# Parameter loads on other queues, wider statistics products, more start-up transposes and an earlier group-A output in a mixer + mixture-of-experts block

## The chip, the core and the metric

The kernel runs on one core of a Trainium2 chip. The metric is device time in microseconds (us) of one execution. A core has five engines that run their own instruction lists in order and wait for each other by semaphores: TensorE (PE, matmuls; its weight loads are shown as PEld), VectorE (DVE), ScalarE (ACT), GpSimd (POOL) and SyncE (SP, which here only issues DMAs). ACT and POOL can issue DMAs too. All DMAs share 16 DMA engines.

## The reference

One encoder layer over 256 tokens of 1024 channels, all in float32. What matters here is the first half, up to the output projection, and that 32 experts' weights (192 MB) have to be read in the second half.

```python
def mixer_block(h, w_in, conv_a_w, conv_b_w, conv_b_bias, ln_b_g, ln_b_b, beta_a, beta_b, w_out):
    proj = jnp.einsum("bsd,dc->bsc", h, w_in)
    a_in, a_b, a_c, b_val, b_gate = jnp.split(proj, ..., axis=-1)
    y_a = a_b * depthwise_conv_centred(a_c * a_in, conv_a_w)          # width 3
    u = b_val * jax.nn.sigmoid(b_gate)
    u = depthwise_conv_centred(u, conv_b_w) + conv_b_bias             # width 31
    y_b = jax.nn.silu(layernorm(u, ln_b_g, ln_b_b))
    y = jnp.concatenate([head_rmsnorm(y_a, N_HEADS_A, beta_a),
                         head_rmsnorm(y_b, N_HEADS_B, beta_b)], axis=-1)
    return jnp.einsum("bsc,cd->bsd", y, w_out)

h = rmsnorm(x, norm_mix_g);  x = x + mixer_block(h, ...)
h = rmsnorm(x, norm_ffn_g);  x = x + hierarchical_moe(h, ...)   # 4 groups of 8 experts, top 1 group, top 2 experts
return rmsnorm(x, norm_final_g)
```

## The kernel before

Channels lie on the 128 partitions, tokens along the free axis, so each of the two groups has four blocks (`b` = 0 to 3) of 128 channels by 256 tokens. The order of every engine's work is the order in which the code is written; nothing is rearranged.

**Weights.** A ring of 25 buffers of 1 MB holds all weights. `stream` lists the transfers in the order of use; `fill()` issues them on SP as long as buffers are free, and `done()` gives buffers back with a rank. Besides the buffers, each DMA of SP and ACT takes the next of eight completion lanes, and waits until the DMA eight places before it has landed.

**Start.** `x` comes in two halves (one DMA on ACT, one on SP). PE turns identity matrices into a scratch tile (line 226, 14 times) and then transposes the 16 blocks of `x` (line 235). The row norm is made by DVE, ACT and two more transposes (line 239), then `keep_busy(15)` issues 15 more identity transposes (line 216) while DVE forms the normalised `hT` (line 243). The parameters of the convolutions and norms (31 rows of `conv_b_w`, 3 of `conv_a_w`, 5 single rows) are loaded into `prow`, which shares memory with `vb`, and are transposed into `prm` by line 388.

**Projections.** `proj()` makes one block: plain float32 for the first (`g` and `v`, line 298), otherwise a split into a high and a low part (lines 302, 303 and 307), for which ACT makes the high parts of the weights (`split_hi`, line 270) and POOL the low ones (`split_lo`, line 276, 10 times). Block order on PE: g0, v0, g1, v1, g2, v2, g3, v3 (group B), then c, i and b of group A.

**Group B's wide convolution** runs on DVE: 31 taps (line 338, one multiply-add each) for every block; for the last block ten of the taps are done by ACT (multiply, line 323) and POOL (add, line 325), handed out by `pool_taps`, and line 342 adds that sum `gsum` at the end. `run_taps(n)` puts the next n taps at that place of DVE's list; two blocks are worked on in turn.

**Group A.** `a_out(b)` multiplies the b projection into `y` on DVE (line 441). `head_stat` squares `y` on ACT (line 451) and sums heads by products with `hsel` (line 455); `a_head` takes root (ACT, line 459) and reciprocal (DVE, line 460) and spreads them (ACT, line 464); `a_scale` turns them on PE (line 472), scales them on ACT (line 510) and multiplies them into `y` on POOL (line 511).

**After the convolution** comes the LayerNorm of group B: mean by products with `onesd` (`mu`, lines 558 to 564; the last waits for line 342), squares, variance (`va`, line 585), root, SiLU, head norm (line 605), and the output projection (lines 631 to 633). Between these steps PE does products of group A's output projection (`more`, line 519), which had been kept for this. Then routing, gathering, and 16 pairs of experts (lines 902 and 941).

The lines that set the order around the change are these:

```python
    a_out(1)
    head_stat(0, 0, True)
    a_conv(3)
    pool_taps(WB - NG + 2, 2)
    run_taps(9)
    head_stat(0, 1, True)
    pool_taps(WB - NG + 4, 3)
    a_out(2, lambda: head_stat(0, 0, False))
    a_head(0, 2)
    run_taps(9)
    a_out(3, lambda: a_scale(0))
    pool_taps(WB - NG + 7, NG - 7)
    split_lo(("out", 2), 71)
```

Of the kernel before, what the change touches and what calls it, by code (L numbers as in the profile page):

```python
# [9 lines left out]
FT = mybir.dt.float32  # L10
# [4 lines left out]
AF = mybir.ActivationFunctionType  # L15
# [4 lines left out]
P = 128  # L20
# [4 lines left out]
NB = CM // P  # L25
# [10 lines left out]
WA, WB = 3, 31  # L36
# [4 lines left out]
def encoder_kernel(ctx, tc, x, norm_mix_g, w_in, conv_a_w, conv_b_w, conv_b_bias, ln_b_g, ln_b_b,  # L41
                   beta_a, beta_b, w_out, norm_ffn_g, w_route_group, b_route_group,
                   w_route_expert, b_route_expert, w1, w3, w2, norm_final_g, out):
    nc = tc.nc
    PE, V, S, G = nc.tensor, nc.vector, nc.scalar, nc.gpsimd

    ring = ctx.enter_context(tc.tile_pool(name="ring", bufs=1))
    cst = ctx.enter_context(tc.tile_pool(name="cst", bufs=1))
    pacc = ctx.enter_context(tc.tile_pool(name="pacc", bufs=1, space=PSUM))
    ps = ctx.enter_context(tc.tile_pool(name="ps", bufs=2, space=PSUM))  # L50
    mixctx = ExitStack()
    mx = mixctx.enter_context(tc.tile_pool(name="mx", bufs=1))
# [26 lines left out]
    for pr, nm in seq[1:]:  # L79
        wv, n = W[nm]  # L80
# [32 lines left out]
    def fill(upto=None, spare=None):  # L113
        spare = keep[0] if spare is None else spare
        while nxt[0] < (len(stream) if upto is None else upto):
            key, src, *part = stream[nxt[0]]
            own = part[0] if part else key
            if own not in shared:
                if len(free) <= spare:
                    break  # L120
                shared[own] = slot(own)
            o = part[1] if part else 0
            tv = shared[own][:, o:o + src.shape[1] * src.shape[2]].rearrange("p (a b) -> p a b", a=src.shape[1])
            nc.sync.dma_start(out=tv, in_=src)
            tiles[key] = tv
            nxt[0] += 1
# [3 lines left out]
    R_B, R_A, R_BIAS, R_LG, R_LB, R_BA, R_BB = 0, WB, WB + WA, WB + WA + 1, WB + WA + 2, WB + WA + 3, WB + WA + 4  # L130
    vb = mx.tile([P, NB, T], FT, name="vb")
    prow = vb.rearrange("p a b -> p (a b)")[0:NPR, 0:CM]
    s1 = slot("s1")
    ub = s1[:, 0:NB * (T + 2 * HALO)].rearrange("p (b t) -> p b t", b=NB)
    n = NB * (T + 2 * HALO)
# [6 lines left out]
    S.dma_start(out=x1[:, 1], in_=xv[:, 1])  # L142
    nc.sync.dma_start(out=x1[:, 0], in_=xv[:, 0])
    S.dma_start(out=g1, in_=norm_mix_g.rearrange("o (p k) -> (o p) k", k=KD))
    fill(1)
    nc.sync.dma_start(out=prow[0:WB], in_=conv_b_w[0])
    nc.sync.dma_start(out=prow[R_A:R_A + WA], in_=conv_a_w[0])
    fill(2)
    for r, a in ((R_BIAS, conv_b_bias), (R_LG, ln_b_g), (R_LB, ln_b_b), (R_BA, beta_a), (R_BB, beta_b)):
        nc.sync.dma_start(out=prow[r:r + 1], in_=a)  # L150
    fill(4)

    epst = cst.tile([P, 1], FT, name="epst")
# [25 lines left out]

    onesd = mx.tile([P, P], FT, name="onesd")  # L180
    V.memset(onesd, 1.0 / CM)
    hsel = cst.tile([P, 2], FT, name="hsel")
    V.memset(hsel, 0.0)
    for a in range(2):
        V.memset(hsel[64 * a:64 * a + 64, a:a + 1], 1.0 / 64.0)
# [12 lines left out]
    gid = cst.tile([P, GRP, EPG], FT, name="gid")  # L198
    G.iota(gid, pattern=[[1, GRP], [0, EPG]], base=0, channel_multiplier=0,
           allow_small_or_imprecise_dtypes=True)  # L200

    def acc_tiles():
        return [[pacc.tile([P, 512], FT, name=f"acc{a}{b}", tag=f"acc{a}{b}") for b in range(2)]
                for a in range(2)]
# [3 lines left out]
    def tmp():  # L208
        ntmp[0] += 1
        return s2[:, ntmp[0] % 8]  # L210


    def keep_busy(n):
        p = ps.tile([P, P], FT, name="dummy", tag="h")
        for _ in range(n):
            PE.transpose(p, ident, ident)
# [5 lines left out]
    r1 = cst.tile([P, 2], FT, name="r1")  # L222
    pt = [t for row in acc_tiles() for t in row]
    prb = ps.tile([P, T], FT, name="prb", tag="mm")
    for _ in range(14):
        PE.transpose(prb[:, 0:P], ident, ident)
    for h in range(2):
        if h:
# [9 lines left out]
    for h in range(2):  # L238
        PE.transpose(prb[:, h * P:(h + 1) * P], r1[:, h:h + 1].to_broadcast([P, P]), ident)
    S.copy(rb, prb)  # L240
    keep_busy(15)
    for k in range(KD):
        V.scalar_tensor_tensor(hT[:, k], pt[k // 2][:, (k % 2) * T:(k % 2) * T + T], g1[:, k:k + 1], rb,
                               op0=OP.mult, op1=OP.mult)
# [22 lines left out]
    def split_hi(key):  # L267
        w = tiles[key]
        h_ = slot(("hi", key), FR, "whi").rearrange("p (a b) -> p a b", a=w.shape[1])
        S.copy(h_, w)  # L270
        hi[key] = h_
# [11 lines left out]
    def proj(name, b, between=None):  # L283
        NPJ[0] += 1
        p = ps.tile([P, T], FT, name="pj", tag=("h", "mm")[NPJ[0] % 2])
        if name in "gv" and b < 2:
            n = [name] * KD
            sl = [(k, slice(0, P)) for k in range(KD)]
        elif name in "gv":
            n = [("in", name, b // 2)] * KD  # L290
            sl = [(k, slice(b % 2 * P, (b % 2 + 1) * P)) for k in range(KD)]
        else:
            n = [("in", name, k // 4) for k in range(KD)]
            sl = [(k % 4, slice(b * P, (b + 1) * P)) for k in range(KD)]
        if b == 0 and name in "gv":
            w = tiles["in", name, 0]
            for k in range(KD):
                PE.matmul(p, w[:, k, 0:P], hT[:, k], start=(k == 0), stop=(k == KD - 1))
            return p
        for k in range(KD):  # L300
            w = hi[n[k]][:, sl[k][0], sl[k][1]]
            PE.matmul(p, w, xhi[:, k], start=(k == 0), stop=False)  # L302
            PE.matmul(p, w, xlo[:, k], start=False, stop=False)  # L303
        if between:
            between()
        for k in range(KD):
            PE.matmul(p, lo[n[k]][:, sl[k][0], sl[k][1]], xhi[:, k], start=False, stop=(k == KD - 1))
        return p
# [131 lines left out]
    def a_out(b, between=None):  # L440
        V.tensor_tensor(y[:, b], proj("b", b, between), y[:, b], op=OP.mult)


    hst, sqh = {}, {}

    def head_stat(g0, b, first):
        if first:
            if b == 0:
                hst[g0] = ps.tile([P, NB, 2, 2], FT, name="hs", tag="mm")
            sqh[b] = tmp()  # L450
            S.activation(sqh[b], y[:, g0 + b], AF.Square)
            return
        for n in (b, b + 1):
            for h in range(2):
                PE.matmul(hst[g0][:, n, h], sqh[n][:, h * P:(h + 1) * P], hsel, start=True, stop=True)

    def head_factor(g0, b0, n, copy):
        rs = mx.tile([P, NB, 2, 2], FT, name="rs", bufs=2)
        S.activation(rs[:, 0:n], hst[g0][:, b0:b0 + n], AF.Sqrt, bias=epst)
        V.reciprocal(rs[:, 0:n], rs[:, 0:n])  # L460
        out_ = []
        for b in range(n):
            rx = tmp().rearrange("p (h a c) -> p h a c", h=2, a=2)
            copy[b](rx, rs[:, b, :, :, None].to_broadcast([P, 2, 2, 64]))
            out_.append(rx)
        return out_
# [50 lines left out]
    def oproj_a(blk, h, nh):  # L517
        w = tiles["out", blk // 2][:, blk % 2, nh * 512:(nh + 1) * 512]
        PE.matmul(accs[h][nh], y[:, blk, h * P:(h + 1) * P], w, start=(blk == 0), stop=False)
# [4 lines left out]
    head_stat(0, 0, True)  # L524
    a_conv(3)
    pool_taps(WB - NG + 2, 2)
    run_taps(9)
    head_stat(0, 1, True)
    pool_taps(WB - NG + 4, 3)
    a_out(2, lambda: head_stat(0, 0, False))  # L530
    a_head(0, 2)
    run_taps(9)
    a_out(3, lambda: a_scale(0))
    pool_taps(WB - NG + 7, NG - 7)
    split_lo(("out", 2), 71)
    done(*both(*B_), "xhi", "xlo", rank=66)
# [10 lines left out]
    for nh in range(2):  # L547
        oproj_a(0, 1, nh)
    head_stat(0, 3, True)
    run_taps(5)  # L550
    head_stat(0, 2, False)
    a_head(2, 2)
    split_hi(("out", 3))
    oproj_a(0, 0, 1)
    oproj_a(1, 1, 0)
# [21 lines left out]
    sqs = ca  # L577
# [1 line left out]
        V.tensor_tensor(vb[:, b], vb[:, b], mu, op=OP.subtract)  # L579
        S.activation(sqs[:, b], vb[:, b], AF.Square)  # L580
    more(2)
    va = ps.tile([P, 2], FT, name="va", tag="mm")
    for h in range(2):
        for b in range(NB):
            PE.matmul(va[:, h:h + 1], sqs[:, b, h * P:(h + 1) * P], onesd[:, 0:1], start=(b == 0), stop=(b == NB - 1))
    more(1)
    rv = mx.tile([P, 2], FT, name="rv")
    S.activation(rv, va, AF.Sqrt, bias=epst)
    S.activation(warm, epst, AF.Silu)
    V.reciprocal(rv, rv)  # L590
    prv = ps.tile([P, T], FT, name="prv", tag="mm")
    for h in range(2):
        PE.transpose(prv[:, h * P:(h + 1) * P], rv[:, h:h + 1].to_broadcast([P, P]), ident)
    more(2)
    hst[NB] = ps.tile([P, NB, 2, 2], FT, name="hs", tag="mm")
    for b in range(NB):
        V.tensor_tensor(vb[:, b], vb[:, b], prv, op=OP.mult)
        S.activation(vb[:, b], vb[:, b], AF.Silu, bias=prm[:, b, R_LB:R_LB + 1],
# [408 lines left out]
    for pr in range(NP - 2):  # L1007
# [7 lines left out]
        a = hidden(pr, meanwhile={} if prev else {("w1", 1): mid})  # L1015
# [28 lines left out]
    a = hidden(NP - 2)  # L1044
# [17 lines left out]
    a = hidden(NP - 1, ("w3",))  # L1062
# [112 lines left out]
```

## Time and profile before

| | us |
|---|---|
| median of 3 runs (571.79 to 572.28) | 572.24 |
| the profiled execution, its own time | 573.68 |
| its span (first to last instruction) | 572.0 |

| engine | busy us | share of the span |
|---|---|---|
| PE | 542.0 | 95% |
| DVE | 175.8 | 31% |
| ACT | 118.7 | 21% |
| POOL | 74.6 | 13% |
| the 16 DMA engines (main queue) | | 95% |

A view of the profile either groups instructions, or lists them in order of time. Each row names engine, line, operation, what is written and read, and in brackets how long the engine had been idle and what released it. The share of busy time is a mean over stages with different limits, so the stages are looked at one by one. "PEclk" is the granted share of TensorE's full clock (1.00 is 2.4 GHz, 0.50 is 1.2 GHz).

### The profile page before, as it was taken

To read this page: it belongs to the slowest core of one execution; us is meant where nothing else is said; L and a number is where in the kernel's file an instruction comes from. 1 tells how busy PE (TensorE), PEld (TensorE's weight loads), DVE (VectorE), ACT (ScalarE), POOL (GpSimd) and SP (SyncE) were. 2 spreads that over 40 slices of the span, in tenths; PEclk is the share of its full clock that TensorE was granted. 3 is DMA by queue.
4 is the path that set the end of the run, shared out by engine and by line. 5 is a ranking of instruction groups with operands and counts; after the bars stand their busy time and mean duration, and the time that the engine had idled before them with its cause. 6 is when DMAs were issued, how large, how long until landed. Compare 5 with 4: busy or idle time off the path is not lost. (4 is left out here: it accounts for less than half of the span.)

```text
span 572.0 us, 7467 instructions
## 1 busy us (share of the span) xinstructions
PE 542.0 (95%) x3017; PEld 293.0 (51%) x3017; DVE 175.8 (31%) x380; ACT 118.7 (21%) x240; POOL 74.6 (13%) x63
## 2 busy tenths in 40 slices
PE   8899989999999999999999999999979997999894
PEld 7899956873363436344443634353426342634363
DVE  4899984572120113021211201120202020200323
ACT  4663655451101000010001010000100110011123
POOL 1699873000000000000000000000000000030001
PEclk9999998999999999999999999999999999999998
DMA  7999967389999999999999999999999999999993
GB/s 238 357 385 408 394 263 275 125 301 388 424 421 422 421 421 422 421 422 420 420 421 421 422 420 422 421 421 422 422 420 420 422 420 422 422 420 419 364 334 105
DMA packets 48778, 218.87 MB, mean 383 GB/s; under 512 B 6062, under 2 KB 19646, under 8 KB 25957
## 3 DMA queue, kind: packets, MB, share of 16 engines
q1 hardware_dynamic: 48452, 217.83, 95.0%
q8 instruction: 25, 0.41, 0.3%
q10 hardware_dynamic: 288, 0.53, 0.3%
q14 instruction: 13, 0.10, 0.0%
HBM read 217.30 MB, written 1.05 MB: 382 GB/s over the span
## 5 line engine op out<-in xcount | busy, mean ns | idle before, releaser
L902 PE MATMUL ph<-wt 128*64 128x512 f32 x1024 | 230.0, 594 | 11.1 <-DMA wt<-in_w_dram 10.2
L902 PEld LDWEIGHTS ph<-wt 128*64 128x64 f32 x1024 | 76.1, 137 | 158.9 <-issue 132.6
L941 PE MATMUL yp<-wt,at 128*64 128x512 f32 x448 | 99.7, 595 | 0.8 <-issue 0.8
L917 DVE SCALAR_TENSOR_TENSOR sl<-ph,fs,sl 128x512 f32<-128x512 f32 x16 | 12.0, 751 | 201.6 <-PE ph L902 188.7
L941 PEld LDWEIGHTS yp<-wt,at 128*64 128x64 f32 x448 | 33.3, 137 | 58.2 <-issue 55.3
L1031 POOL TENSOR_TENSOR wt<-x2h,x2l 128x1024 f32<-128x1024 f32 x2 | 4.7, 2384 | 388.6 <-PE yp L941 388.6
L338 DVE SCALAR_TENSOR_TENSOR csum<-wt,prm,csum 128x256 f32<-128x256 f32 x106 | 51.8, 489 | 3.4
L931 DVE TENSOR_TENSOR yl<-yp,yh 128x512 fp32r<-128x512 f32 x28 | 19.4, 692 | 94.9 <-ACT yh L930 94.9
L276 POOL TENSOR_TENSOR wlo<-wt,whi 128x2048 fp32r<-128x2048 f32 x10 | 45.8, 4625 | 12.7 <-ACT whi L270 12.7
L930 ACT CAST yh<-yp 128x512 fp32r<-128x512 f32 x28 | 16.4, 586 | 134.1 <-PE yp L941 134.1
L915 ACT ACTIVATE sl<-ph,fs 128x512 f32<-128x512 f32 x16 | 11.0, 687 | 101.7 <-PE ph L902 101.7
L302 PE MATMUL pj<-xhi,whi 128*128 128x256 f32 x128 | 31.4, 283 | 0.0
L303 PE MATMUL pj<-xlo,whi 128*128 128x256 f32 x128 | 31.4, 283 | 0.0
L872 ACT CAST gw<-gwp 128x256 fp32r<-128x256 f32 x16 | 5.9, 373 | 108.2 <-PE gwp L870 108.2
L823 PE MATMUL gp<-gt,x2h 128*128 128x256 f32 x112 | 23.6, 292 | 1.8 <-ACT fs L884 1.8
L302 PEld LDWEIGHTS pj<-xhi,whi 128*128 128x128 f32 x128 | 24.6, 192 | 0.0
L303 PEld LDWEIGHTS pj<-xlo,whi 128*128 128x128 f32 x128 | 24.6, 192 | 0.0
L824 DVE TENSOR_TENSOR wt<-gp,g 128x512 f32<-128x512 f32 x28 | 19.4, 692 | 15.3 <-PE gp L823 15.3
L952 PE MATMUL acc<-yh,gw 128*128 128x512 f32 x56 | 23.7, 424 | 0.0
L952 PE MATMUL acc<-yl,gw 128*128 128x512 f32 x56 | 22.1, 395 | 0.0
L823 PE MATMUL gp<-gt,x2l 128*128 128x256 f32 x112 | 22.0, 278 | 0.0
L270 ACT CAST whi<-wt 128x2048 fp32r<-128x2048 f32 x10 | 18.9, 1905 | 3.1 <-DMA wt<-in_w_in_dram 3.1
(239 smaller groups left out, 505.4 us busy)
## 6 DMA issues: line engine op xcount, KB each, us to landing
wt<-in_w_dram SPq DMA_DIRECT2D x178, 1024.0 KB, 19.8
wt<-in_w_dram SPq DMA_DIRECT2D x26, 512.0 KB, 10.2
wt<-in_w_in_dram SPq DMA_DIRECT2D x10, 1024.0 KB, 10.0
wt<-in_w_out_dram SPq DMA_DIRECT2D x4, 1024.0 KB, 12.8
wt<-in_w_dram SPq DMA_DIRECT2D x4, 256.0 KB, 6.1
out_dram<-wt SPq DMA_DIRECT2D x3, 256.0 KB
wt<-in_x_dram SPq DMA_DIRECT2D x1, 512.0 KB
wt<-in_x_dram ACTq DMA_DIRECT2D x1, 512.0 KB
```

The lines of the kernel that those rows point to most:

```text
L270: S.copy(h_, w)
L276: eng.tensor_tensor(l_, w, hi[key].bitcast(FT), op=OP.subtract)
L302: PE.matmul(p, w, xhi[:, k], start=(k == 0), stop=False)
L303: PE.matmul(p, w, xlo[:, k], start=False, stop=False)
L338: V.scalar_tensor_tensor(a if j < last else vb[:, b], ub[:, b, j:j + T], w(j), a, op0=OP.mult, op1=OP.add)
L823: PE.matmul(p[:, k], xs[:, h, 2 * q + k], g[:, h], start=(n == 0), stop=(n == 3))
L824: V.tensor_tensor(xg[:, 2 * q:2 * q + 2], p, g2[:, 2 * q:2 * q + 2, None].to_broadcast([P, 2, 4 * CAP]), op=OP.mult)
L902: PE.matmul(p[e * CAP:(e + 1) * CAP], xg[:, k, c0 + e * CAP:c0 + (e + 1) * CAP], w, start=(k == 0), stop=(k == KD - 1))
L930: S.copy(yh, p)
L931: V.tensor_tensor(yl, p, yh.bitcast(FT), op=OP.subtract)
L941: PE.matmul(pn[nh][e * CAP:(e + 1) * CAP], at[:, k, e * CAP:(e + 1) * CAP], w[:, k % 2, nh * 512:(nh + 1) * 512], start=(k == 0), stop=(k ...
L952: PE.matmul(accm[h][nh], gw[:, h], y, start=(pr == 0 and n == 0), stop=(pr == NP - 3 and n == 1))
```

## The change

1. The parameter rows no longer go over SP. `conv_b_w` and `conv_a_w` are issued by ACT after its half of `x`, the five single rows by POOL after its index tables.
2. 22 identity transposes instead of 14 stand ahead of `x`, and 6 instead of 15 behind the norm.
3. `hsel` has 32 columns instead of 2 (30 of zeros), so that the head statistics are products of 32 columns, and the variance takes 64 columns of `onesd` instead of 1; only the columns of before are read.
4. Group A's third and fourth outputs change places with taps: the root and reciprocal for blocks 0 and 1 now stand in front of `a_out(2)`'s multiply with six taps ahead of them, `a_out(3)` follows two taps behind `a_out(2)`, one of POOL's taps moves behind it, and the taps left over move behind the second `a_head`.

```diff
-    fill(1)
-    nc.sync.dma_start(out=prow[0:WB], in_=conv_b_w[0])
-    nc.sync.dma_start(out=prow[R_A:R_A + WA], in_=conv_a_w[0])
     fill(2)
-    for r, a in ((R_BIAS, conv_b_bias), (R_LG, ln_b_g), (R_LB, ln_b_b), (R_BA, beta_a), (R_BB, beta_b)):
-        nc.sync.dma_start(out=prow[r:r + 1], in_=a)
+    S.dma_start(out=prow[0:WB], in_=conv_b_w[0])
+    S.dma_start(out=prow[R_A:R_A + WA], in_=conv_a_w[0])
     fill(4)
...
-    hsel = cst.tile([P, 2], FT, name="hsel")
+    hsel = mx.tile([P, 32], FT, name="hsel")
...
+    for r, a in ((R_BIAS, conv_b_bias), (R_LG, ln_b_g), (R_LB, ln_b_b), (R_BA, beta_a), (R_BB, beta_b)):
+        G.dma_start(out=prow[r:r + 1], in_=a)
...
-    for _ in range(14):
+    for _ in range(22):
         PE.transpose(prb[:, 0:P], ident, ident)
...
-    keep_busy(15)
+    keep_busy(6)
...
-                hst[g0] = ps.tile([P, NB, 2, 2], FT, name="hs", tag="mm")
+                hst[g0] = ps.tile([P, NB, 2, 32], FT, name="hs", tag="mm")
...
     pool_taps(WB - NG + 2, 2)
-    run_taps(9)
+    run_taps(6)
     head_stat(0, 1, True)
-    pool_taps(WB - NG + 4, 3)
-    a_out(2, lambda: head_stat(0, 0, False))
-    a_head(0, 2)
-    run_taps(9)
+    pool_taps(WB - NG + 4, 2)
+    a_out(2, lambda: (head_stat(0, 0, False), a_head(0, 2), run_taps(3)))
+    pool_taps(WB - NG + 6, 1)
+    run_taps(2)
     a_out(3, lambda: a_scale(0))
+    run_taps(4)
     pool_taps(WB - NG + 7, NG - 7)
...
     head_stat(0, 3, True)
-    run_taps(5)
     head_stat(0, 2, False)
     a_head(2, 2)
+    run_taps(8)
...
-    va = ps.tile([P, 2], FT, name="va", tag="mm")
+    va = ps.tile([P, 2, 64], FT, name="va", tag="mm")
...
-            PE.matmul(va[:, h:h + 1], sqs[:, b, h * P:(h + 1) * P], onesd[:, 0:1], start=(b == 0), stop=(b == NB - 1))
+            PE.matmul(va[:, h], sqs[:, b, h * P:(h + 1) * P], onesd[:, 0:64], start=(b == 0), stop=(b == NB - 1))
```

How the instructions stand now, at three places. First DVE, from the taps behind `a_out(1)` to the end of the convolution (`csum` is the running sum of a block's taps, `vb` its result, `rs` the head norms, L441 an `a_out`). Before:

```order
L338 SCALAR_TENSOR_TENSOR csum<-wt,prm,csum 128x256 x9
L441 TENSOR_TENSOR hT<-pj,hT 128x256
L460 RECIPROCAL rs<-rs 128x8
L338 SCALAR_TENSOR_TENSOR csum<-wt,prm,csum 128x256 x9
L441 TENSOR_TENSOR hT<-pj,hT 128x256
L338 SCALAR_TENSOR_TENSOR csum<-wt,prm,csum 128x256 x3
L338 SCALAR_TENSOR_TENSOR vb<-wt,prm,csum 128x256
L338 SCALAR_TENSOR_TENSOR csum<-wt,prm,csum 128x256
L460 RECIPROCAL rs<-rs 128x8
L338 SCALAR_TENSOR_TENSOR csum<-wt,prm,csum 128x256 x2
L338 SCALAR_TENSOR_TENSOR vb<-wt,prm,csum 128x256
L342 TENSOR_TENSOR vb<-vb,hT 128x256
```

And after, where six taps stand ahead of the first row shown:

```order
L460 RECIPROCAL rs<-rs 128x8
L338 SCALAR_TENSOR_TENSOR csum<-wt,prm,csum 128x256 x3
L441 TENSOR_TENSOR hT<-pj,hT 128x256
L338 SCALAR_TENSOR_TENSOR csum<-wt,prm,csum 128x256 x2
L441 TENSOR_TENSOR hT<-pj,hT 128x256
L338 SCALAR_TENSOR_TENSOR csum<-wt,prm,csum 128x256 x4
L460 RECIPROCAL rs<-rs 128x8
L338 SCALAR_TENSOR_TENSOR csum<-wt,prm,csum 128x256 x6
L338 SCALAR_TENSOR_TENSOR vb<-wt,prm,csum 128x256
L338 SCALAR_TENSOR_TENSOR csum<-wt,prm,csum 128x256 x3
L338 SCALAR_TENSOR_TENSOR vb<-wt,prm,csum 128x256
L342 TENSOR_TENSOR vb<-vb,hT 128x256
```

The number of taps is the same, 26 from `a_out(1)` on; the second reciprocal stood three taps ahead of L342 and now stands eleven ahead of it.

Second ACT, the same stretch, from the first root (L459) to the second (L323 are multiplies for POOL's taps, L510 the scales of `a_scale(0)`, L451 the squares of blocks 2 and 3). Before:

```order
L323 ACTIVATE hT<-wt,prm 128x256 x3
L459 ACTIVATE rs<-hs,epst 128x8
L464 COPY wt<-rs 128x256 x2
L510 ACTIVATE wt<-hb,prm 128x256 x2
L323 ACTIVATE hT<-wt,prm 128x256 x3
L451 ACTIVATE wt<-hT 128x256
L545 COPY g2s<-pg 128x8
L546 COPY bb<-pg 128x40
L451 ACTIVATE wt<-hT 128x256
L459 ACTIVATE rs<-hs,epst 128x8
```

And after:

```order
L323 ACTIVATE hT<-wt,prm 128x256 x2
L459 ACTIVATE rs<-hs,epst 128x8
L464 COPY wt<-rs 128x256 x2
L323 ACTIVATE hT<-wt,prm 128x256
L510 ACTIVATE wt<-hb,prm 128x256 x2
L323 ACTIVATE hT<-wt,prm 128x256 x3
L451 ACTIVATE wt<-hT 128x256
L546 COPY g2s<-pg 128x8
L547 COPY bb<-pg 128x40
L451 ACTIVATE wt<-hT 128x256
L459 ACTIVATE rs<-hs,epst 128x8
```

One multiply has moved behind the copies; the two scales, the last three multiplies, both squares and the second root stand in the order of before.

Third SP, the start (`vb` is `prow`, the parameter rows). Before:

```order
L143 DMA wt<-in_x_dram 128x1024
L124 DMA wt<-in_w_in_dram 128x8x256
L146 DMA vb<-in_conv_b_w_dram 31x512
L147 DMA vb<-in_conv_a_w_dram 3x512
L124 DMA wt<-in_w_in_dram 128x8x256
L150 DMA vb<-in_conv_b_bias_dram 1x512
L150 DMA vb<-in_ln_b_g_dram 1x512
L150 DMA vb<-in_ln_b_b_dram 1x512
L150 DMA vb<-in_beta_a_dram 1x512
L150 DMA vb<-in_beta_b_dram 1x512
L124 DMA wt<-in_w_in_dram 128x8x256 x2
```

And after:

```order
L143 DMA wt<-in_x_dram 128x1024
L124 DMA wt<-in_w_in_dram 128x8x256 x4
L124 DMA wt<-in_w_in_dram 128x4x512
L173 DMA g_99<-in_norm_ffn_g_dram 128x8
L124 DMA wt<-in_w_in_dram 128x4x512
```

The seven parameter loads have left SP's list, and five weight transfers stand behind its half of `x` without anything between.

## Rows read from the trace of the kernel before

**Rows 1.** Busy time by stage: us, PE, PEld, DVE, ACT, POOL, PEclk, DMA share, GB/s

```profile
100.00:113.00 13.00, 13.00 (x72) 10.82 (x71) 6.49 (x18) 5.28 (x17) 0.00 (x0) 1.00 0.36 126
127.00:572.00 445.00, 421.94 (x2226) 188.94 (x2222) 79.99 (x147) 48.37 (x109) 6.28 (x4) 1.00 0.99 405
```

**Rows 2.** Waits of PE and of SP's queue, whole run: total us, times, longest

```profile
PE ph L902 <- DMA wt<-in_w_dram: 10.2, 10, 1.4
...
SPq L124 <- PE acc L632: 11.0, 1, 11.0
...
SPq L124 <- DMA vb<-in_conv_b_w_dram: 2.7, 1, 2.7
```

**Rows 3.** DVE in 20.1 to 84.2 us, grouped, and DVE's start of it

```profile
L338 DVE SCALAR_TENSOR_TENSOR csum<-wt,prm,csum 128x256 f32<-128x256 f32 x106 | 51.8, 489 | 3.4
...
20.17 0.42 DVE L373 TENSOR_TENSOR wt<-pj,wt 128x256 f32<-128x256 f32 x1 [2.26 <-PE pj L298]
```

**Rows 4.** Timeline of the start, PE: start, duration, line, operation, count, idle before

```profile
1.43 3.25 PE L226 MATMUL prb<-ident 128*128 128x128 f32 x14 [1.43 <-POOL ident masks.py:199]
5.63 3.56 PE L235 MATMUL acc<-ident,wt 128*128 128x128 f32 x16 [0.95 <-DMA wt<-in_x_dram]
...
9.24 1.80 PE L216 MATMUL dummy<-ident 128*128 128x128 f32 x15
10.88 3.62 PE L298 MATMUL pj<-hT,wt 128*128 128x256 f32 x16
15.98 0.41 PE L388 MATMUL pp<-ident,vb 39*128 39x39 f32 x4 [1.48 <-ACT gvh L261]
16.32 3.72 PE L298 MATMUL pj<-hT,wt 128*128 128x256 f32 x16
```

**Rows 5.** The start on SP's queue and ACT, and the DMA share by stretch

```profile
9.01 0.22 SPq L150 DMA_DIRECT2D vb<-in_beta_b_dram  x1
11.92 1.26 SPq L124 DMA_DIRECT2D wt<-in_w_in_dram  x2
...
14.52 1.04 ACT L261 CAST gvh<-wt 128x1024 fp32r<-128x1024 f32 x1 [0.37 <-DMA wt<-in_w_in_dram]
...
12.00:13.00 1.00, 1.00 (x6) 0.90 (x5) 1.00 (x4) 0.59 (x1) 0.00 (x0) 1.00 0.07 24
```

**Rows 6.** Timeline of 72 to 85 us, by engine

```profile
73.64 0.74 PE L472 MATMUL hb<-ident,wt 128*128 128x128 f32 x4 [1.43 <-ACT wt L464]
...
72.96 0.19 DVE L460 RECIPROCAL rs<-rs 128x8 f32<-128x8 f32 x1
80.43 0.20 DVE L460 RECIPROCAL rs<-rs 128x8 f32<-128x8 f32 x1
...
77.11 0.51 ACT L323 ACTIVATE hT<-wt,prm 128x256 f32<-128x256 f32 x1 [1.06 <-POOL hT L325]
79.18 0.27 ACT L459 ACTIVATE rs<-hs,epst 128x8 f32<-128x8 f32 x1 [0.70 <-PE hs L455]
...
74.98 1.42 POOL L511 TENSOR_TENSOR hT<-hT,wt 128x256 f32<-128x256 f32 x2 [2.64 <-ACT wt L510]
76.35 2.34 POOL L325 TENSOR_TENSOR hT<-hT 128x256 f32<-128x256 f32 x3
78.65 4.54 POOL L276 TENSOR_TENSOR wlo<-wt,whi 128x2048 fp32r<-128x2048 f32 x1
```

**Rows 7.** Timeline: DVE additions of two SBUF tiles

```profile
82.19 1.28 DVE L342 TENSOR_TENSOR vb<-vb,hT 128x256 f32<-128x256 f32 x1
...
91.03 1.68 DVE L603 TENSOR_TENSOR wt<-vb 128x256 f32<-128x256 f32 x4
```

**Rows 8.** The clock: PE's timeline of 91 to 98 us, and busy time by stretch

```profile
91.51 1.95 PE L605 MATMUL hs<-hsel,wt 128*128 128x2 f32 x16
...
95.94 1.90 PE L472 MATMUL hb<-ident,wt 128*128 128x128 f32 x8
...
94.30:97.60 3.30, 3.30 (x11) 2.16 (x10) 1.02 (x4) 0.71 (x3) 0.00 (x0) 0.50 0.60 246
```

More of the change, by code (lines that the diff above doesn't have):

```diff
@@ L458, in head_factor @@
         rs = mx.tile([P, NB, 2, 2], FT, name="rs", bufs=2)
-        S.activation(rs[:, 0:n], hst[g0][:, b0:b0 + n], AF.Sqrt, bias=epst)
+        S.activation(rs[:, 0:n], hst[g0][:, b0:b0 + n, :, 0:2], AF.Sqrt, bias=epst)
         V.reciprocal(rs[:, 0:n], rs[:, 0:n])
@@ L581, in encoder_kernel @@
     more(2)
-    va = ps.tile([P, 2], FT, name="va", tag="mm")
+    va = ps.tile([P, 2, 64], FT, name="va", tag="mm")
     for h in range(2):
         for b in range(NB):
-            PE.matmul(va[:, h:h + 1], sqs[:, b, h * P:(h + 1) * P], onesd[:, 0:1], start=(b == 0), stop=(b == NB - 1))
+            PE.matmul(va[:, h], sqs[:, b, h * P:(h + 1) * P], onesd[:, 0:64], start=(b == 0), stop=(b == NB - 1))
     more(1)
     rv = mx.tile([P, 2], FT, name="rv")
-    S.activation(rv, va, AF.Sqrt, bias=epst)
+    S.activation(rv, va[:, :, 0], AF.Sqrt, bias=epst)
     S.activation(warm, epst, AF.Silu)
@@ L594, in encoder_kernel @@
     more(2)
-    hst[NB] = ps.tile([P, NB, 2, 2], FT, name="hs", tag="mm")
+    hst[NB] = ps.tile([P, NB, 2, 32], FT, name="hs", tag="mm")
     for b in range(NB):
```

## The prediction

> **What bounds the kernel now.** I read the busy time by stage first. From 127 us to the end the DMA engines are at 0.99 and PE waits 10.2 us in all for expert weights: that stage moves a fixed number of bytes, and ends so much earlier or later as it starts [rows 1, 2]. What starts it is the mixer. Between 100 and 113 us the DMA share is 0.36, and SP sits 11.0 us on a wait for the output projection (L632), because all ring buffers are full [rows 1, 2]. So weights that arrive earlier before that wait gain nothing, and a shift of the compute chain up to the output projection goes to the end one for one.
>
> That chain is DVE's between 20 and 83 us. It starts when the second projection (v0) is done: DVE had idled 2.26 us for it and starts at 20.17. From there it runs tap behind tap: 106 taps take 51.8 us with 3.4 us between them, one every 0.52 us, with no wait on another engine [rows 3]. The last step, L342, starts at 82.19 and ends at 83.47 [rows 7]; the mean `mu` and everything behind follow from it. I therefore cost the change at three places: when v0 ends, when L342 ends, and what PE's clock does between there and the output projection.
>
> **Start-up (parameter queues, 22 transposes).** The first projection starts behind the 15 dummies, at 10.9, and ends at 14.5. PE then idles 1.48 us in front of the parameter transposes (L388) and starts v0 at 16.32 [rows 4]. The idle time is put down to ACT, but ACT's row of that name is a cast that L388 does not read; the five single rows are what it does read, and SP issued the last of them at 9.01, behind v0's megabyte [rows 5]. With these on POOL that wait goes. What is late next is v0's weight: ACT's cast of it starts at 14.52, released by its DMA [rows 5]. So v0 cannot start much before 14.55, and the most that this part can give is 16.32 - 14.55 = 1.8 us.
>
> It will give less. In 12 to 13 us the DMA share is 0.07, one sixteenth: a single engine is at work, and SP's next weight went out at 11.92, after 2.7 us of waiting for `conv_b_w` to land [rows 2, 5]. I read this as the 31 rows going through one of the 16 engines, behind the first weight, g0, which had landed by 9.01 (the single row issued then had to wait for it) [rows 5]. That transfer thus takes 11.92 - 9.01 = 2.9 us of one engine. On ACT's queue it no longer stands behind g0 but beside it, and if the engine serves both in turn, g0 lands up to 2.9 us later, at 9.0 to 11.9. PE needs g0 for its first projection. With 11.6 taken: 11.6 + 3.7 for the projection + 0.4 for L388 = 15.7 to 15.8, against 16.32. I take **-0.5 us**; the ends are -1.8 (g0 not delayed) and +1.7 (PE waits two to three us for g0 and its clock falls, priced below).
>
> The transposes themselves are paid in this shadow. The 14 take 0.22 us each and end before `x`; eight more fill the 0.95 us of idle time and run about 0.5 us past it [rows 4]. The 16 of `x` also go at 0.22 us, the dummies behind them at 0.11: PE's pace doubled at about 9 us, from what 1.2 GHz gives to what 2.4 GHz gives, after nothing but transposes (PEclk shows 1.00 on both sides, so the spacing is the evidence) [rows 4]. If it doubles before `x` now, 16 x 0.11 = 1.8 us are saved. Between +0.5 and -1.8 us on a step that then waits for g0, I take nothing. TensorE: Matmul & The Clock Gate (the Trainium skill, "Part 4: PE-mode transpose") says that transposes don't count as work that raises the clock; by that the eight extra ones could only delay, by the same 0.5 us, but the rows disagree with it.
>
> **Group A's order: a new wait on DVE.** The second reciprocal (L460) stood three taps ahead of L342 and now stands eleven ahead. DVE reaches it 8 x 0.52 = 4.2 us earlier, at 80.43 - 4.2 = 76.25 [rows 6]. Its operand doesn't get there that early. It comes from ACT's second root (79.18, ends 79.45), which stands behind the squares, which stand behind the last of POOL's tap multiplies (77.11); that one idled 1.06 us for POOL's first of three adds (76.35), and the adds stand behind L511 (74.98), which waited for `a_scale(0)` [rows 6]. None of this order has changed. What moves is its head: the first reciprocal, from 72.96 to three taps and one multiply earlier, 72.96 - 1.9 = 71.05. ACT's copies then end at 72.0 instead of 73.9. PE can turn them at once, but no earlier than it is free, and it was free 1.43 us before 73.64, so the turn moves by 1.4 to 1.6 us [rows 6]. With 1.6: L511 at 73.4, the adds at 74.75, ACT's last multiply at 75.5, the root at 77.6 to 77.85. The reciprocal waits from 76.25 to 77.85, **+1.6 us**, and the 11 taps and L342 queue behind it. L342 starts at 82.19 + 1.6 = 83.8. PE's waits for `a_out` don't enter: b3's projection ends at about 73.6, and DVE asks for it at 73.9.
>
> **What L342 then meets.** L342 adds two SBUF tiles. The same shape takes 1.68 / 4 = 0.42 us in L603, with POOL idle, and took 1.28 us at 82.19, when POOL was in a `split_lo` (78.65 + 4.54 = 83.19); it ended 0.28 us after that [rows 6, 7]. So it was held up by POOL. In the new order POOL runs from the same adds: adds at 74.75, `split_lo` of out 2 at 78.65 - 1.6 = 77.05 to 81.6, the two L511 to 82.9 (ACT's scales for them are ready by 81.1: reciprocal 77.9, copies to 78.8, a cast of 1.9, the first scale), then `split_lo` of out 3 from 82.9 to 82.9 + 4.54 = 87.45. L342 arrives at 83.8, 0.9 us into it. Both times hang on the same add, so the 0.9 does not depend on the 1.6.
>
> If L342 waits for that instruction as it did for the other, it ends at 87.45 + 0.28 = 87.7, against 83.47: **+4.2 us** with the wait above in it. If it only runs slower beside POOL, and takes its 1.28 us again, it ends at 83.8 + 1.28 = 85.1, +1.6 us. One row cannot tell these apart; I take the first, because the end at a fixed 0.28 us behind POOL's needs no rate. SBUF — State Buffer (the Trainium skill, "Who interferes with whom") says the same: a VectorE instruction with two SBUF inputs contends with a GpSimd instruction that reads SBUF, and whoever issued second fully blocks. By that rule the term is +4.2, by sharing +1.6; the row agrees with both.
>
> **The clock behind it.** PE has nothing to do between the product with the third block (about 82.2) and L342's end at 87.7: 5.5 us, more than three times its longest idle time so far (1.48 us, after which the clock stayed at 1.00). Before, the clock fell to 0.50 after 1.95 us of two-column products, and stayed there for 94.3 to 97.6, where 3.4 us of work took the place of 1.7 [rows 8]. I expect it to fall here, at the price of one such stretch, **+1.7 us** (0 if it holds; 3.4 if two follow each other).
>
> **Wider products.** 16 products of two columns start every 0.11 us, and the eight transposes of 128 columns at half clock every 0.21, thus 0.11 at full clock [rows 8]: the pitch is not set by the columns, and 32 or 64 cost nothing. If they keep the clock up at 94 us, the fall there goes, **-1.7 us**; if not, 0. The profiled execution took 1.44 us more than the median of the runs (573.68 against 572.24), so part of them may not have had it at all. I take -1.7.
>
> **The rest costs nothing.** b3 ends 1.5 us earlier and gives its buffers back, but SP only comes to its 11.0 us wait earlier. ACT's two issues (0.6 and 1.2 us, as on SP) end before its first use of `x` at 5.8, POOL's five before its first `split_lo` at 19.9.
>
> **The sum.** -0.5 + 4.2 + 1.7 - 1.7 = +3.7 us. Against the profiled execution, 573.7 + 3.7 = 577.4 (span 575.7); against the median, 572.24 + 3.7 = **575.9**.
>
> **Rivals.** (1) DVE doesn't wait, since the chain over POOL is shorter than I read it: L342 comes before `split_lo` of out 3, takes 0.42 to 1.28 us, and the sum is -0.5 - 0.4 - 1.7 = -2.6, **569.6** (to 568.3 with the whole start-up gain). It decides at the reciprocal: the root would have to end by 76.2. The row of before speaks against it: three engines' steps in a row, each with its idle time named. (2) The wait is there, but L342 shares with POOL: -0.5 + 1.6 - 1.7 = -0.6, **571.6**; if 2.8 us of idle PE lower the clock, 573.3. (3) The widening doesn't do what it is for, and the clock falls there as before: likeliest sum without the -1.7, **577.6**. (4) The start-up loses: g0 late, PE idle at the very start, clock at half through the first projection, +1.7 instead of -0.5, **578.1**.
>
> **How the numbers follow.** Likeliest case 0.36; (3) 0.20; (4) 0.07; (2) 0.17; (1) 0.20. The two sides lie apart: above, the likeliest case with (3) and (4) runs from 574.6 (start-up at its best) to 579.3 (start-up at its worst, nothing gained at 94 us); below, (1) and (2) run from 568.3 to 573.3. The range leaves out about half of (1) and the top of the upper side: 569.4 to 578.6. Faster or slower by over 0.2% (1.1 us, what a measurement of this kernel can tell from no change) means below 571.1 or above 573.4. Faster: (1) and a little of (2), 0.25. Same: most of (2), 0.12. Slower: 0.63.
>
> **What would show it.** L460's second instance idle 1.6 us in front, released by ACT; L342 with about 3.9 us instead of 1.28, ending with POOL's L276; PEclk at 0.50 soon after it; 1.00 around the head statistics; L388 without idle time in front, v0 at 15.8, g0's first user waiting for a DMA. I am wrong if the reciprocal does not wait, or if L342 gets through beside POOL.

## The result, and the profile after

| | before | after |
|---|---|---|
| median of 5 runs, us | 572.28 (571.79 to 572.88) | 578.38 (577.72 to 578.89) |
| profiled execution, us (span) | 573.68 (572.0) | 577.72 (576.0) |

The ratio is 1.0104 [1.0089, 1.0119]: 1% slower. Executions of one kernel differ with TensorE's mean granted clock (runs of the kernel before in the whole record: 571.6 to 572.6 us at 0.993 to 0.997, 576.4 to 577.4 us at 0.985 to 0.988), so lowest times and profiles stand beside the medians.

The start after the change (timeline: start, duration, engine, line, operation, count, idle before and what ended it; answers [rows 4, 5] and DVE's row of [rows 3]):

```profile
1.43 4.95 PE L226 MATMUL prb<-ident 128*128 128x128 f32 x22 [1.43 <-POOL ident masks.py:199]
6.17 2.00 PE L235 MATMUL acc<-ident,wt 128*128 128x128 f32 x16
11.59 3.69 PE L298 MATMUL pj<-hT,wt 128*128 128x256 f32 x16 [2.54 <-DMA wt<-in_w_in_dram]
15.21 0.44 PE L388 MATMUL pp<-ident,vb 39*128 39x39 f32 x4
15.58 3.72 PE L298 MATMUL pj<-hT,wt 128*128 128x256 f32 x16
...
19.44 0.42 DVE L373 TENSOR_TENSOR wt<-pj,wt 128x256 f32<-128x256 f32 x1 [1.07 <-ACT whi L270]
```

The parameter transposes no longer wait, the first projection does: PE idles 2.54 us for the first weight. DVE starts at 19.44 instead of 20.17, 0.73 us earlier. The blocks of `x` take 2.00 us instead of 3.56; PE has doubled its pace before them, and nothing is gained by it.

The stretch from 73 to 105 us, by engine (answers [rows 6, 7]; lines from about 530 on are one higher than before):

```profile
76.95 0.20 DVE L460 RECIPROCAL rs<-rs 128x8 f32<-128x8 f32 x1 [1.42 <-ACT rs L459]
82.84 3.99 DVE L342 TENSOR_TENSOR vb<-vb,hT 128x256 f32<-128x256 f32 x1
...
82.04 4.50 POOL L276 TENSOR_TENSOR wlo<-wt,whi 128x2048 fp32r<-128x2048 f32 x1
...
86.88 1.22 PE L565 MATMUL mu<-vb,onesd 128*128 128x256 f32 x2 [5.48 <-DVE vb L342]
87.90 4.60 PE L519 MATMUL acc<-wt,hT 128*128 128x512 f32 x6
92.33 1.90 PE L586 MATMUL va<-onesd,hT 128*128 128x64 f32 x16
...
97.20 1.97 PE L606 MATMUL hs<-hsel,wt 128*128 128x32 f32 x16
...
103.86 0.80 PE L632 MATMUL acc<-whi,yhl 128*128 128x512 f32 x1
```

And busy time by stretch (us, PE, PEld, DVE, ACT, POOL, PEclk, DMA share, GB/s; answers [rows 1, 8]):

```profile
84.80:91.60 6.80, 4.72 (x7) 2.47 (x8) 3.44 (x5) 1.45 (x4) 2.61 (x2) 0.50 0.91 343
94.30:97.60 3.30, 3.17 (x12) 1.33 (x11) 2.30 (x8) 3.27 (x7) 0.00 (x0) 1.00 0.01 2
...
127.00:574.00 447.00, 425.49 (x2250) 193.84 (x2250) 83.29 (x154) 48.52 (x110) 6.29 (x4) 1.00 0.99 405
```

Three of these steps before the change, from its timeline:

```profile
83.53 0.70 PE L564 MATMUL mu<-vb,onesd 128*128 128x256 f32 x2 [0.40 <-DVE vb L342]
...
86.64 1.84 PE L585 MATMUL va<-onesd,hT 128*128 128x1 f32 x16
...
99.84 0.79 PE L631 MATMUL acc<-whi,yhl 128*128 128x512 f32 x1
```

Read down the path, after against before: DVE's start -0.73; the end of L342 +3.36 (86.83 against 83.47), thus 4.09 us lost on DVE; the variance product +5.69 (92.33 against 86.64), 2.33 us more, lost at half clock; the head sums +5.69 still (97.20 against 91.51 [rows 8]); the output projection +4.02 (103.86 against 99.84), since the fall of [rows 8] is not there after; the end +4.0. The DMA-bound stage is as it was, and SP's wait for the output projection is 11.0 us as in [rows 2]. So the two profiled executions differ by 4.04 us, and each part of it has its place. The medians differ by 6.10: the profiled execution of before lay 1.40 above its median, that of after 0.66 below.

### The profile page after: what moved, and what is told of

Read it like the earlier page. It is cut to its first block, busy times and chain, and to the rows that moved or that the text cites. A ratio compares the mean times of both kernels' runs of the same rounds, so it can differ in the third digit from the quotient of the medians.

```text
span 576.0 us, 7470 instructions
## 1 busy us (share of the span) xinstructions
PE 541.4 (94%) x3016; PEld 294.5 (51%) x3016; DVE 178.6 (31%) x380; ACT 118.6 (21%) x240; POOL 77.3 (13%) x68
## 5 line engine op out<-in xcount | busy, mean ns | idle before, releaser
L931 ACT CAST yh<-yp 128x512 fp32r<-128x512 f32 x28 | 16.4, 587 | 134.2 <-PE yp L942 134.2
```

## The experiments

The theory is that group A's order makes the loss: DVE waits for the reciprocal, L342 then has to wait for POOL's subtraction, and PE's idle time lowers its clock. Its rivals are that the loss sits in the start-up or the wider products, that L342 only shares with POOL, and that the clock falls for another reason. All kernels were timed in five rounds against the kernel before.

| kernel | lowest, median, highest us (runs) | ratio to before |
|---|---|---|
| a_order_alone | 577.7, 578.78, 579.93 (6) | 1.0096 [1.0061, 1.0131] |
| b_order_undone | 571.51, 572.50, 574.20 (12) | 0.9978 [0.9952, 1.0004] |
| c_wide_alone | 571.75, 572.29, 575.71 (12) | 0.9983 [0.9959, 1.0006] |
| d_start_alone | 571.07, 572.26, 574.83 (12) | 0.9991 [0.9970, 1.0012] |
| e_split8 | 572.83, 576.51, 580.06 (12) | 1.0050 [1.0021, 1.0079] |
| f_recip_late | 570.95, 572.09, 573.48 (12) | 0.9969 [0.9947, 0.9991] |
| h_fill_gap | 575.50, 577.48, 579.38 (9) | 1.0053 [1.0023, 1.0083] |
| i_conv_pool | 575.09, 575.85, 576.98 (12) | 1.0046 [1.0028, 1.0064] |
| j_both | 568.42, 568.74, 570.60 (6) | 0.9929 [0.9901, 0.9956] |
| k_fill_start | 570.85, 571.12, 571.96 (12) | 0.9961 [0.9939, 0.9983] |
| l_conv_pool_old_order | 569.57, 569.86, 570.91 (9) | 0.9948 [0.9930, 0.9966] |
| m_narrow | 568.81, 569.27, 570.46 (8) | 0.9930 [0.9901, 0.9958] |

The kernel before had medians of 572.69 (a to d), 572.91 (e to i) and 572.91 (j to m) beside them. The last column is not the ratio of the medians: in each of the three groups the kernel before has five to seven runs of 576.4 to 577.4 us.

### Which part makes the loss

**Group A's order alone** (part 4 of the diff, on the kernel before).

> The kernel before with group A's new order alone. Theory 1 (the order makes the whole loss): DVE waits 1.4 us at the second reciprocal, L342 then meets POOL's split of out 3 and takes 4.0 us instead of 1.28, ends 4.1 us later than before; PE idles 5.5 us, its clock falls to 0.50 for 6.8 us and costs 2.3 us up to the variance products: 572.3 + 4.1 + 2.3 = 578.7 us. Theory 2 (the order costs only the part that the profiles show net, with the narrow products free): 572.3 + 4.1 = 576.4. Rival (the loss sits in the start-up or in the wider products): 572 to 573.

The median is 578.78, as theory 1 has it. The DVE part of its timeline repeats that of after:

```profile
77.62 0.20 DVE L460 RECIPROCAL rs<-rs 128x8 f32<-128x8 f32 x1 [1.39 <-ACT rs L459]
83.52 4.01 DVE L342 TENSOR_TENSOR vb<-vb,hT 128x256 f32<-128x256 f32 x1
...
87.58 1.22 PE L565 MATMUL mu<-vb,onesd 128*128 128x256 f32 x2 [5.51 <-DVE vb L342]
...
92.28 1.84 PE L586 MATMUL va<-onesd,hT 128*128 128x1 f32 x16
...
84.00:90.80 6.80, 3.22 (x5) 1.85 (x6) 4.94 (x5) 1.44 (x4) 4.11 (x2) 0.50 0.91 337
```

L342 ends at 87.53, 4.06 us later than before. In 84.0 to 90.8 us the granted clock is 0.50 (last row); in 93 to 101 it is 1.00, although the products are narrow. One number of the expectation did not come: from L342's end to the variance product it is 4.75 us (92.28 - 87.53) against 3.17 before, so the clock cost 1.58 us in this execution and not 2.3. The stretch is as long as after the change, but only 3.3 us of it lie behind L342's end, where they were 4.8 (to 91.6, from 86.83).

**The order put back** (parts 1 to 3 alone).

> The changed kernel with group A's order put back; the start-up and the wider products stay. Theory 1: no wait at the reciprocal, L342 ends 0.7 us earlier than in the kernel before, no fall of the clock in 80 to 100 us: 572.3 - 0.7 = 571.6 us. Theory 2 (the wider products are worth one clock stretch in every run): 572.3 - 0.7 - 1.7 = 569.9. Rival (the loss sits outside the order): 576 to 578.

The profiled execution (571.51) is theory 1's: no wait at the reciprocal, L342 1.27 us, and the last mean product 0.74 us earlier than in the kernel before:

```profile
82.79 0.70 PE L564 MATMUL mu<-vb,onesd 128*128 128x256 f32 x2 [0.39 <-DVE vb L342]
```

Five of its 12 runs lie between 571.5 and 571.9; the others, up to 574.2, made the median 572.50. Parts 1 to 3 lose nothing. Why their runs spread was tried on another kernel (k below).

**The wider products alone** (part 3) and **the start-up alone** (parts 1 and 2).

> The kernel before with the wider products alone. Theory 1: most runs of the kernel before don't have the fall of the clock at 94 us that its profile shows (that execution took 1.4 us more than the median), so the median stays at 572.3 (572.0 to 572.6) and what goes are runs near 573.7; mean granted clock 0.997 in all runs. Theory 2: the fall is in every run and goes: 570.6. Theory 3: width does nothing, the profile shows the fall at 94 us again in some of the runs.

> The kernel before with the start-up part alone (parameter queues, 22 and 6 transposes). Theory 1: DVE starts its taps 0.7 us earlier and that goes to the end: 572.3 - 0.7 = 571.6 us, PE idle 2.5 us for the first weight. Rival (a shift of the start is absorbed before the output projection, or the clock behind 80 us changes): 572.3 or more.

The widening's median is 0.4 us lower (572.29 against 572.69), and the interval of its ratio holds no change; theory 2's 570.6 lies below its lowest run. The mean granted clock of 0.997 in all runs did not come: it is 0.989 to 0.997. The start-up's median is 0.4 us lower as well, again with an interval that holds no change; six of its 12 runs lie between 572.5 and 574.9. The 0.7 us expected there are not in its profiled execution (571.64) either, whose DVE starts 0.29 us earlier than before:

```profile
19.88 0.42 DVE L373 TENSOR_TENSOR wt<-pj,wt 128x256 f32<-128x256 f32 x1 [1.07 <-ACT whi L270]
```

What the widening's profiled execution (575.71) shows is something else, a start that the kernel before can have too, since that part of it is untouched:

```profile
5.48 2.06 PE L235 MATMUL acc<-ident,wt 128*128 128x128 f32 x16 [0.80 <-DMA wt<-in_x_dram]
...
15.85 0.62 PE L388 MATMUL pp<-ident,vb 39*128 39x39 f32 x4 [2.96 <-ACT gvh L261]
16.40 6.69 PE L298 MATMUL pj<-hT,wt 128*128 128x256 f32 x16
```

PE doubled its pace early, was done early, idled 2.96 us, and its second projection took 6.69 us instead of 3.72, with the granted clock at 0.50:

```profile
15.60:22.40 6.80, 6.55 (x18) 5.34 (x19) 1.34 (x2) 5.02 (x4) 2.60 (x1) 0.50 1.08 365
```

In the kernel before, 7 of 29 runs beside this one took 576.5 to 577.3. Their mean granted clock is 0.985 to 0.988, against 0.989 in this execution and 0.991 to 0.997 in the other 22, so that they are of this kind is likely, but none of them was profiled.

### What L342 waits for

**POOL's subtraction in eight pieces.**

```diff
-    split_lo(("out", 3), 78)
+    split_lo(("out", 3), 78, n=8)     # eight subtractions of 128x256
```

> The changed kernel with POOL's split of out 3 cut into eight instructions of 128 elements by 2 rows each (4.5 us becomes 8 of about 0.6). Theory 1 (a VectorE addition of two SBUF tiles waits for the one POOL instruction that runs, and no longer): L342 takes at most 0.6 + 0.42 = 1.0 us, ends at about 83.8 instead of 86.8, PE idles 2.5 us instead of 5.5 and the clock stays at 1.00: 578.4 - 3.0 - 2.3 = 573.1 us. Theory 2 (the two share the port and L342 only runs slower): L342 takes 1.3 us or more, whatever the pieces. Theory 3 (POOL keeps the port until its queue is empty): L342 takes 4 us again, 578.4.

L342 took 0.89 us instead of 3.99:

```profile
82.69 0.72 POOL L276 TENSOR_TENSOR wlo<-wt,whi 128x256 fp32r<-128x256 f32 x1
82.80 0.89 DVE L342 TENSOR_TENSOR vb<-vb,hT 128x256 f32<-128x256 f32 x1
83.37 0.90 POOL L276 TENSOR_TENSOR wlo<-wt,whi 128x256 fp32r<-128x256 f32 x1
...
83.74 0.70 PE L565 MATMUL mu<-vb,onesd 128*128 128x256 f32 x2 [2.38 <-DVE vb L342]
...
88.55 1.89 PE L586 MATMUL va<-onesd,hT 128*128 128x64 f32 x16
```

It ended at 83.69, 0.28 us behind the piece that ran when it came (82.69 + 0.72 = 83.41), and the next piece was held up in its turn, 0.90 us. Before, after, and in a and h it ended 0.28 to 0.29 us behind the whole subtraction. With sharing (theory 2) it would have taken 1.3 us or more, whatever the pieces. So this addition waits for the one POOL instruction that runs, and theory 1 is shown. SBUF — State Buffer (the Trainium skill, "Who interferes with whom") says that whoever issued second is blocked; the traces agree, in both directions.

On the clock this expectation was wrong. Behind PE's 2.38 us of idle time it fell in the profiled execution (574.48):

```profile
84.70:88.00 3.30, 3.30 (x5) 1.35 (x4) 1.19 (x4) 1.45 (x4) 3.30 (x6) 0.50 0.66 278
```

Only one run, 572.83, is near the 573.1 that I wrote. The runs spread over 7 us, some above the changed kernel itself. Their mean granted clock goes with it, from 0.996 at 572.83 over 0.991 at 574.48 to 0.982 at 580.06, so the longer runs spent more time at half clock; where in the run, and why this kernel more than the others, is not explained.

**The reciprocal three taps ahead of L342 again.**

```diff
-    a_head(2, 2)
     run_taps(8)
+    a_head(2, 2)
```

> The changed kernel with the second reciprocal put behind the eight taps, three taps ahead of L342 as in the kernel before. Theory 1: the reciprocal doesn't wait, L342 starts at 81.5 us, where POOL is between its first split (ends 80.7) and the next multiplies, takes 0.42 us, and ends 1.5 us earlier than in the kernel before; no fall of the clock: 572.3 - 1.5 = 570.8 us. Theory 2 (L342 meets POOL's multiplies, 0.7 us each): 571.5. Rival (the loss is in the rest of the new order): 574 or more.

Five of 12 runs lie at 570.95 to 571.33, as theory 1 has it. From its profiled execution (573.39):

```profile
11.83 5.38 PE L298 MATMUL pj<-hT,wt 128*128 128x256 f32 x16 [2.85 <-DMA wt<-in_w_in_dram]
...
81.55 0.20 DVE L460 RECIPROCAL rs<-rs 128x8 f32<-128x8 f32 x1
83.32 0.42 DVE L342 TENSOR_TENSOR vb<-vb,hT 128x256 f32<-128x256 f32 x1
```

No wait, and L342 at 0.42 us while POOL idles. This one moved line is worth about 6 us (578.38 to 572.09), so the whole loss hung on it. The execution also suggests why the other runs are longer: PE idled 2.85 us for the first weight, the granted clock is 0.50 in 13.0 to 16.4 us, and the first projection took 5.38 us instead of 3.69.

### The clock as a term of its own

**PE kept busy in the gap of 5.5 us.**

```diff
+    keep_busy(48)
     PE.matmul(mu, onesd, vb[:, NB - 1], start=False, stop=True)
```

> The changed kernel with 48 identity transposes on PE (5.2 us at 0.11) in front of the last mean product, where it idles 5.5 us; nothing else moves. Theory 1 (the idle time makes the clock fall, and that is a term of its own): granted clock 1.00 from 7 us to the end's stretch, L342 still 4.0 us, and 1.6 to 2.3 us less: 576.1 to 576.8. Rival (the clock falls for another reason, or its fall costs nothing): 578.4.

```profile
83.12 5.40 PE L216 MATMUL dummy<-ident 128*128 128x128 f32 x48
88.82 0.70 PE L565 MATMUL mu<-vb,onesd 128*128 128x256 f32 x2 [0.30 <-DVE vb L342]
...
91.93 1.89 PE L586 MATMUL va<-onesd,hT 128*128 128x64 f32 x16
```

```profile
83.00:93.00 10.00, 9.70 (x69) 7.90 (x67) 6.97 (x9) 1.44 (x4) 6.35 (x4) 1.00 0.94 366
```

The granted clock (last row, PEclk) stays at 1.00. L342 ends at 88.77 and the variance starts 3.16 us later; after the change it was 86.83 and 5.50 us. The difference, 2.34 us, is the clock's price in that execution, within 0.01 of what the two timelines gave. The lowest run is 2.2 us under that of the changed kernel, the median only 0.9, less than the 1.6 to 2.3 expected. The profiled execution (577.51, at the median) had the slow first projection again (5.38 us, PE idle 3.08 us ahead of it); whether the other runs near the median had it is not shown.

### The start

**The convolution parameters on POOL's queue.**

```diff
-    S.dma_start(out=prow[0:WB], in_=conv_b_w[0])
-    S.dma_start(out=prow[R_A:R_A + WA], in_=conv_a_w[0])
...
+    G.dma_start(out=prow[0:WB], in_=conv_b_w[0])      # ahead of the five single rows
+    G.dma_start(out=prow[R_A:R_A + WA], in_=conv_a_w[0])
```

> The changed kernel with the two convolution parameters issued on POOL's queue ahead of the five single rows, instead of ACT's. Theory 1 (on ACT's queue the 31 rows take one DMA engine from the first weight; POOL's queue cuts rows in sixteen): the first weight lands 1.5 to 2.5 us earlier, the first projection starts at 9.5 to 10 instead of 11.6, DVE starts its taps at 17.6 to 18.0 instead of 19.4: 578.4 - 1.6 = 576.8 us. Theory 2 (the rows delay it there too, or land too late for the parameter transposes): 578.4 or more.

```profile
9.96 3.69 PE L298 MATMUL pj<-hT,wt 128*128 128x256 f32 x16 [0.83 <-DMA wt<-in_w_in_dram]
...
17.81 0.42 DVE L373 TENSOR_TENSOR wt<-pj,wt 128x256 f32<-128x256 f32 x1 [0.83 <-PE pj L298]
...
81.21 3.98 DVE L342 TENSOR_TENSOR vb<-vb,hT 128x256 f32<-128x256 f32 x1
...
89.89 1.89 PE L586 MATMUL va<-onesd,hT 128*128 128x64 f32 x16
```

The first projection started 1.6 us earlier, DVE started 1.63 us earlier, and the median is 2.5 us lower than after the change, more than the shift. Of the rest this timeline shows 0.8 us: from L342's end (85.19) to the variance it is 4.70 us, so the clock cost 1.53 us here and 2.33 after the change (0.3 us of it are lost again up to the end of the span, 573.9 against 576.0). All 12 runs lie within 1.9 us. How the 34 rows travel is seen in the trace's packets: on ACT's queue 34 of 2048 bytes, one behind the other (two at most at any moment) from 5.85 to 10.0 us; on POOL's 19, most of 4096 bytes, up to ten at a time in 6.4 to 7.6 us. The trace doesn't name the engine of a packet, so that it is one engine on ACT's queue is read from the packets' following each other. What I had written of how POOL's queue cuts the rows was wrong; that it spreads them was right. DMA: Bandwidth & Descriptors (the Trainium skill, "Why a DMA increments its semaphore by 16 and not by 1") says that the number of engines, up to 16, has to divide the transfer's outer size, which leaves one for 31 rows, and that GpSimd's queue gives some copies all 16 with the rows shared out; the packets agree with both (31 rows are 15 packets of two rows and one of one row).

**PE kept busy until the first weight** (on f_recip_late: `keep_busy(28)` instead of 6 behind `x`).

> The changed kernel with the late reciprocal, and 28 dummy transposes behind x instead of 6, so that PE is busy nearly until the first weight lands. Theory (the upper half of the late reciprocal's runs, 572.0 to 573.5, is a fall of the clock during the first projection, after 2.5 to 3 us of idle PE): nearly all runs at 571.0 to 571.4, first projection 3.7 us and not 5.4. Rival (those runs have another cause): 571 to 573.5 again.

```profile
8.09 3.22 PE L216 MATMUL dummy<-ident 128*128 128x128 f32 x28
11.76 3.69 PE L298 MATMUL pj<-hT,wt 128*128 128x256 f32 x16 [0.45 <-DMA wt<-in_w_in_dram]
```

All 12 runs lie at 570.85 to 571.96, where f's reached 573.48, with the first weight as late as ever. So the upper half of f's runs goes with the idle time in front of the first projection.

### Together

**Late reciprocal and POOL's queue**, the same **with group A's old order**, and the same **with narrow products** (the widening undone).

> The two edits that each took a loss away, together: the second reciprocal behind the eight taps, and the convolution parameters on POOL's queue. Theory (the two terms add, and no idle time of PE is left that lowers its clock): the best runs of the late reciprocal alone (571.0) less 1.6 us: 569.4 us, in nearly all runs, against 572.9. Rival (the gain at the start is absorbed, or POOL's issues come in its way): 571.

> The changed kernel with group A's order put back and the convolution parameters on POOL's queue. Theory 1 (what the new order is worth, once its reciprocal doesn't wait, is L342 beside an idle POOL, 0.42 instead of 1.28 us): 571.6 - 1.6 = 570.0 us, 0.6 to 0.9 above the version with both edits. Theory 2 (the new order is worth nothing): 569.4, the same as that one.

> The version with both edits, with the statistics products at one and two columns as in the kernel before. Theory 1 (the width costs nothing and keeps the clock up in some runs): the same lowest time, 569.4, and a few runs 1.5 to 2 us above it, with the granted clock at 0.50 for 3.4 us between 85 and 100 us. Theory 2 (the width does nothing): the same times, no such runs. Theory 3 (the width is worth 1.7 us in every run): 571.

Both edits together give 568.74, 0.7% under the kernel before and 0.7 us under the 569.4 expected; that surplus is not accounted for. Both losses are gone from the profiled execution:

```profile
9.77 3.69 PE L298 MATMUL pj<-hT,wt 128*128 128x256 f32 x16 [0.69 <-DVE hT L243]
...
77.81 0.20 DVE L460 RECIPROCAL rs<-rs 128x8 f32<-128x8 f32 x1
79.57 0.43 DVE L342 TENSOR_TENSOR vb<-vb,hT 128x256 f32<-128x256 f32 x1
...
80.05 0.70 PE L565 MATMUL mu<-vb,onesd 128*128 128x256 f32 x2
```

With the old order it is 569.86: there L342 takes 1.27 us beside POOL and ends at 80.91 instead of 80.00, and the difference of 1.1 us in the medians is a little more than that. The earlier outputs of group A are worth that much, through POOL's schedule and not through DVE's. The narrow version's median is 0.5 us higher, with intervals that overlap; three of its 8 runs and one of the wide version's 6 lie above 570. Neither theory 1 nor 2 is settled by so few runs; theory 3 is out.

## Where the prediction was right, and where not

The forecast was 575.9 with a range from 569.4 to 578.6; the median is 578.38, at its upper end. The direction and the mechanism were right, the size was too low by 2.5 us, and it is the width of the range, made for the rivals, that holds the time by 0.2 us. One of its ends was added up wrongly: the upper side, with the start at its worst and nothing gained at 94 us, reaches 572.24 + 1.7 + 4.2 + 1.7 = 579.8 and not 579.3. Step by step:

- **Start-up, -0.5:** -0.73 in the profiled pair, -0.29 in d's profile. The first weight was late, as read from the idle DMA engines: ACT began to cast it at 11.48, PE to multiply by it at 11.59 (11.6 said). Rival (4), slow first projection behind a PE that waits for it, was given 0.07 as a case of all runs; it is real, but a matter of single executions (f's and h's profiles show it; with k's transposes in the gap it is not there).
- **The reciprocal's wait, +1.6:** 1.42 [1.39 to 1.42 in after and a], released by ACT as said. Rival (1), no wait, did not come; f shows that it takes the eight taps in front of the reciprocal.
- **L342, together +4.2:** 4.09. It came 0.80 us into POOL's subtraction (0.9 said) and ended 0.29 us behind it (0.28 said). Rival (2), sharing, is refuted by the 3.99 us (1.28 said for it) and by e.
- **The clock behind it, +1.7:** 2.33 in the profile of after, but 1.58 and 1.53 in those of a and i. I priced one stretch of 3.4 us from [rows 8]; the stretches were 6.8 us long in all three, the end that I had given as 3.4 us of loss, of which not all lay on the path. What counts is how much of the stretch is left when L342 ends: 4.8, 3.3 and 3.2 us, and 3.4 in e with its short stretch (1.69 us lost). In each the loss is about half of that. So this term was too small by 0.6 for the profiled pair, by luck about right for a and i, and it is not one number per kernel.
- **Wider products, -1.7:** the step that failed. In the profiled pair the difference is there, 1.67 us between the head sums and the output projection. But the sum was then put on the median of before, and the median does not have that fall as far as the times show: the profiled execution took 1.44 us more, which I saw, wrote down, and still took the whole gain. Nor is the widening shown to take the fall away: the profiles of a, d and m, with narrow products, have none there (granted clock 1.00 in 93 to 101 us of a, in 80 to 100 us of d and m), and the widening alone moved nothing. For the median this term is 0. The others, as the profiles show them, add up to between -0.7 + 4.1 + 1.5 = +4.9 and -0.3 + 4.1 + 2.3 = +6.1, against +6.1 measured; whether some of its five runs also had a slow first projection is not shown. That was rival (3), by another route.
- **The rest at nothing, and one for one to the end:** both held. SP's wait for the output projection is 11.0 us before and after, the stage behind it moves as a block.

## What to carry to other kernels

Moving an instruction up a list does not move its operand: walk the chain behind the operand to the first thing that really comes earlier, and count what is queued behind the wait. Then ask which instruction of another engine the delayed work now meets; here 1.4 us of waiting became 4.1 because an addition arrived 0.8 us after POOL had begun a subtraction of 4.5 us. And if a profiled execution lies above the median, a loss that only it shows is no gain to be taken from the median.

## What the runs showed of the hardware that I had not expected

- The length of PE's idle time did not decide alone whether the clock falls. Behind 2.38 us (e, at 83 us), 2.85, 2.96 and 3.08 us (f, c, h, at the start) it fell; behind 2.54, 2.56 and 2.64 us at the start (after, e, d) it did not. Stretches at 0.50 lasted some 6.8 us in the profiles of after, a, c and i, some 3.4 us in those of before, e, f and h.
- Identity transposes kept the clock up as well: at 1.00 behind 48 of them in the gap at 83 us (h), and a first projection of 3.69 us behind 28 (k), where idle time in their place was followed by 0.50 (after) and by 5.38 us (f).
- The 31 rows of parameters (62 KB), sent one packet behind the other, held the first projection up by 1.6 us (after against i); in the profiles of f and h, where the clock then fell, that projection took 1.7 us longer on top (5.38 instead of 3.69).
- The POOL instruction that follows is held up by VectorE's addition as well: 0.90 us instead of 0.72 for the next piece (e), and 0.91 instead of 0.73 for the multiply behind the whole subtraction (L562 after, L561 before).
